# Holding weight casts behind convolution taps, value copies and the last head's scaling

## The chip, the cores and the metric

The kernel runs on one core of one Trainium2 chip. Its engines are TensorE (PE in the profile; PEld is its loading of stationary operands), VectorE (DVE), ScalarE (ACT), GpSimd (POOL) and SyncE (SP), each with its own queue of instructions, worked off in the order in which the program was laid out. The metric is the device time of one execution in microseconds (us): the median of three runs.

## The reference

One transformer-like block over 512 tokens of width 1024, in float32. After a root-mean-square norm, one large product with `w_in` gives the inputs of two mixers:

```python
qkv = jax.nn.silu(causal_depthwise_conv(jnp.concatenate([qa, ka, va], axis=-1), conv_a))
oa = chunk_gated_delta_rule(qa, ka, va, beta, g)            # 8 heads, keys of 128, values of 256
ya = (rmsnorm(oa, norm_a) * silu(za)) @ w_br_a
ob = chunk_retention(rotary(qb), rotary(kb) * (B_DK ** -0.5), vb)   # 4 heads, keys of 256, values of 512
yb = (rmsnorm(ob, norm_b) * silu(gb)) @ w_br_b
x = x + rmsnorm((sigmoid(gate_a) * ya + sigmoid(gate_b) * yb) @ w_out, n_mix_post)
hn = rmsnorm(x, n_mlp_pre)
return x + rmsnorm(jnp.square(relu(hn @ w_up)) @ w_down, n_mlp_post)
```

The convolution has four taps per channel: a channel's output is the sum of its last four inputs, each times a tap.

## The kernel before, in words

**Products in three parts.** Every large product takes both operands as a high part and a low part. A weight tile arrives from HBM by DMA as `raw` (128 x 1024, 512 KB, on SP's queue). `split_weights` (lines 152 to 164) turns it into `whi`, a cast on ScalarE (line 159), and `wlo`, what is left, a subtraction on VectorE (line 160). TensorE then makes three matmuls per pair of tiles: high by high, high by low, low by high. `raw` has two buffers (four in the stage of the second mixer), `whi` and `wlo` three each, so a cast waits for the DMA of its own load and for TensorE to be done with the load three before it. A "load" below is one such tile with its cast, its subtraction and its 24 matmuls of 512 columns.

**Who orders what.** Programs are written as if in sequence. A scheduler then lays each engine's queue out ahead of time, by readiness in its own model of time and by priority; `tc.high_priority(n)` moves an instruction n places forward. Weight casts and subtractions have 700 in the stage of the first mixer (`AHEAD`) and 200 elsewhere, the convolution's instructions 600 (`CONV_PRIO`), the recurrence 900. `tc.issue_after(ins)` puts the instructions of its block that run on the same engine as `ins` behind `ins` in that queue; instructions on other engines are not touched, and no semaphore is added. On TensorE most instructions of the first mixer keep the order of the program, which a small hand-written clock (`Clock`) lays out: chains of small work by due time, with the large products as fillers between.

**First mixer, about 40 to 480 us.** Fillers make keys, values, queries and gates from `w_in`. `product_features` uses two loads for two PSUM tiles of 128 channels by 512 tokens; when a tile's last matmul is made, `conv_silu` (line 917) takes it: tap 3 on ScalarE (line 923) from PSUM, taps 2, 1, 0 on VectorE (line 926), which also read PSUM, so that the bank comes free after the last of them; then Silu or Tanh. There are 8 tiles of keys, 16 of values and 8 of queries. The first four key tiles are made before the first load of the second four is split. Around that, base inverses of triangular blocks run on VectorE (lines 1081 and 1089), and the recurrence over four chunks per pair of heads alternates TensorE with VectorE (line 1359) and ScalarE (line 1375).

**Second mixer, about 480 to 880 us.** Per head, `scores` makes queries and keys and the scores; `values` makes value and gate with seven products of half-size blocks in place of eight (`seven`). `value` splits a row tile of the values: copy of the high part on ScalarE (line 1715), low part on VectorE (line 1716). `outputs` multiplies scores by values: 30 matmuls into four PSUM tiles over three banks, each read by line 1745 (VectorE) and line 1746 (ScalarE), and scales the four row tiles by the inverse norm (line 1751, ScalarE). The next head begins with the loads of its queries. After the last head, `gate_unit` runs another seven products for the second gate; between them `last_features` transposes the last head's output.

**Rest.** Output product, then the feed-forward part, again with seven products per block.

The functions that the change touches, and what calls them:

Of the kernel before, what the change touches and what calls it, by code (L numbers as in the profile page):

```python
# [14 lines left out]
AF = mybir.ActivationFunctionType  # L15
ALU = mybir.AluOpType
# [48 lines left out]
def hybrid_block_kernel(ctx: ExitStack, tc: tile.TileContext, a: dict, out: bass.AP):  # L65
    nc = tc.nc
# [9 lines left out]
    trickle, later_adds = [], []  # L76
    triples = []
    before, spent, queued, clocks = [None], [None], [JOBS_FROM], []
    ahead = [200]
    marks = []  # L80
    act = ctx.enter_context(tc.tile_pool(name="act", bufs=2))
    sm = ctx.enter_context(tc.tile_pool(name="sm", bufs=2))
# [69 lines left out]
    def split_weights(raw, n, nk, keep=None, ahead=200):  # L152
        if keep is None:
            hi = ring.tile([P, 1024], F32R, tag="whi", name="whi")
            lo = ring.tile([P, 1024], F32R, tag="wlo", name="wlo")
        else:
            hi, lo = keep
        with tc.high_priority(ahead):
            nc.scalar.copy(hi[:, :n], raw[:, :n])  # L159
            nc.vector.tensor_tensor(lo[:, :n], raw[:, :n], hi[:, :n], ALU.subtract)  # L160
# [325 lines left out]
    with tc.tile_pool(name="xp", bufs=2) as xp:  # L486
# [16 lines left out]
        for _ in range(2):  # L503
            w = act.tile([P, 2, D], F32R, tag="og", name="keep")
# [412 lines left out]
    def conv_silu(ps, ch, y, th=None):  # L917

        def tap(j):
            return convw[:, j * 32 + ch : j * 32 + ch + 1]  # L920

        with tc.high_priority(CONV_PRIO):
            nc.scalar.activation(y, ps, AF.Copy, scale=tap(3))
            for j in (2, 1, 0):
                s = 3 - j
                nc.vector.scalar_tensor_tensor(y[:, s:T], ps[:, 0 : T - s], tap(j), y[:, s:T], ALU.mult, ALU.add)  # L926
            if th is None:
                with tc.issue_after(exps[-1].ins):
                    nc.scalar.activation(y, y, AF.Silu, scale=2.0)
            else:  # L930
                nc.scalar.activation(th, y, AF.Tanh)
                nc.vector.scalar_tensor_tensor(y, th, 1.0, y, ALU.add, ALU.mult)
# [595 lines left out]
    with tc.tile_pool(name="pb", bufs=1) as pb_:  # L1528
# [180 lines left out]
            add(1, 0, a, new=True)  # L1709

        def values(h):
            vs, gs = [], []

            def value(t, p):
                nc.scalar.copy(vs[0][t], p)
                nc.vector.tensor_tensor(vs[1][t], p, vs[0][t], ALU.subtract)

            def gate(t):
                nc.scalar.activation(gs[0][:, t, :], gs[0][:, t, :], AF.Silu)

            parts = values_and_gates(vg_sums[h], gs, value, gate)
            next(parts)
            yield
            pairs = [[pb_.tile([P, 2, T], F32R, tag=f"vr{i}{x}", name="vr") for x in "ab"] for i in range(2)]
            vs += [[w[:, t, :] for w in pair for t in range(2)] for pair in pairs]
            gs.append(pb_.tile([P, 4, T], F32, tag="kr", name="gs"))
            for _ in parts:
                pass
            yield vs, gs[0]

        def outputs(scs, vs, gs):
            o = pb_.tile([P, 4, T], F32, tag="qr", name="o")
            ss = pb_.tile([P, 4], F32, tag="oss", name="oss")
            for j in (3, 2, 1, 0):
                ps = psx.tile([P, T], F32, tag="dl", name="dl", bufs=3)
                for i in range(j + 1):
                    js = slice((j - i) * P, (j - i + 1) * P)
                    mm3(
                        ps,
                        (scs[i][0][:, js], scs[i][1][:, js]),  # L1740
                        (vs[0][i], vs[1][i]),
                        i == 0,
                        i == j,
                    )
                nc.vector.tensor_tensor(o[:, j, :], ps, gs[:, j, :], ALU.mult)
                nc.scalar.activation(tmp("osq"), ps, AF.Square, accum_out=ss[:, j : j + 1])
            v = pb_.tile([P, 4], F32, tag="ov", name="ov")
            nc.vector.tensor_scalar(v, ss, 1.0 / 512, EPS, ALU.mult, ALU.add)
            rstd = rsqrt(v, 4, "b")
            for t in range(4):  # L1750
                nc.scalar.mul(o[:, t, :], o[:, t, :], rstd[:, t : t + 1])
            return Rows(None, lambda t, f: o[:, t, f * P : (f + 1) * P])

        def gate_unit(sums, gated, tag, between=None):
# [11 lines left out]
                if between:  # L1766
                    between(i)

        rows = None
        for h in range(4):  # L1770
            vals = values(h)
            scs = scores(h, rows, vals)
# [14 lines left out]
            rows = outputs(scs, *next(vals))  # L1787

        ya, gates, og = [], [], []
        for i in range(2):  # L1790
# [14 lines left out]
        def last_features(i):  # L1805
            if i == 0:
                og.extend(act.tile([P, 4, T], F32R, tag="og", name="og") for _ in range(2))
                return
            f = i - 1
            ps = psx.tile([P, 4, P], F32, tag="tr", name="tr", bufs=1)  # L1810
            with tc.issue_after(triples[-1].ins):
                for t in range(4):
# [387 lines left out]
```

## Time and profile before

| | us |
|---|---|
| median of three runs | 1322.16 (1319.62 to 1323.54) |
| profiled execution | 1322.3 |
| its span, first to last instruction | 1320.5 |
| TensorE busy | 1302.7 |
| VectorE busy | 928.1 |
| ScalarE busy | 698.3 |
| GpSimd busy | 114.5 |
| cast `whi` (line 159), one | 1.05 |
| subtraction `wlo` (line 160), one | 1.22 |

The page gives busy time, the chain of work that ended last and the costliest groups. The timeline has one row per instruction or run of equal instructions: start, time, engine, line, operation, out<-in, and in brackets the idle time of the engine just before it with what ended it. The chain in order of time has rows of start, time and what. The view of windows has a row per stretch: its length, then busy time of PE, PEld, DVE, ACT, POOL with the number of instructions, granted clock, share of the DMA engines and GB/s. TensorE's matmuls overlap, so the row of one lasts longer than its share of the pace; the pace is read from a run of many.

### The profile page before, as it was taken

Reading aid. Unit: us, or ns where it says so; the run is one execution under the profiler, and the core shown is the slowest. Engines: PE = TensorE matmul, PEld = TensorE weight load, DVE = VectorE, ACT = ScalarE, POOL = GpSimd, SP = SyncE. Lnnn points to the kernel's source line nnn. Section 1 sums busy time; section 2 is a strip of 40 time slices with the busy share of each in tenths; the row PEclk is TensorE's granted clock in tenths of the full one; section 3 lists DMA queues with packets and bytes.
Section 4 is the critical chain, followed back from the end, with each engine's and each line's share of the span. In section 5 each row is a group of like instructions: output and inputs, shape, how many; then the busy total and the mean of one; then the engine's idle time right before and its main releaser. Section 6 shows DMA issues by size and latency. Waiting matters only on the chain.

```text
span 1320.5 us, 17594 instructions
## 1 busy us (share of the span) xinstructions
PE 1302.7 (99%) x6555; PEld 1078.3 (82%) x6555; DVE 928.1 (70%) x1554; ACT 698.3 (53%) x1216; POOL 114.5 (9%) x119
## 2 busy tenths in 40 slices
PE   9999999999999999999999999999999999999997
PEld 7888787888888888878888888888889888888886
DVE  6889757486666567768769869769585736648478
ACT  5784546555533524555555554565266646355364
POOL 2101000000101100000010010100001110101001
PEclk9999999999999999999999999999999999999999
DMA  5336452466867867996895896875538895967335
GB/s 193 134 97 159 129 128 64 106 171 184 223 157 185 184 177 219 318 248 181 220 281 160 247 261 184 234 237 159 191 111 242 193 268 144 256 184 182 111 122 133
DMA packets 124149, 243.60 MB, mean 184 GB/s; under 512 B 7638, under 2 KB 39552, under 8 KB 123808
## 3 DMA queue, kind: packets, MB, share of 16 engines
q1 hardware_dynamic: 99808, 183.00, 42.7%
q0 software_dynamic: 21936, 53.12, 23.8%
q10 hardware_dynamic: 2320, 6.36, 1.3%
q8 instruction: 51, 0.84, 0.3%
q14 instruction: 34, 0.28, 0.1%
HBM read 237.20 MB, written 78.66 MB: 239 GB/s over the span
## 4 chain that ended last, share of the span: by engine, by line
PE 86%; DVE 6%; ACT 4%; DMA 2%; issue 1%; DVEq 0%; ACTq 0%
PE mm L692 17%; PE mm L340 16%; PE dl L340 15%; PE mm L97 8%; PE mm L95 8%; PE mm L96 8%; PE dl L692 5%; PE tr L421 1%; DVE wlo L160 1%; DMA raw<-in_w_in_dram 1%; PE tr L701 1%; PE dl L96 1%; PE dl L95 1%; PE dl L97 1%; PE mm L656 1%
## 5 line engine op out<-in xcount | busy, mean ns | idle before, releaser
L160 DVE TENSOR_TENSOR wlo<-raw,whi 128x1024 fp32r<-128x1024 f32 x230 | 281.0, 1223 | 187.9 <-ACT whi L159 187.0
L159 ACT CAST whi<-raw 128x1024 fp32r<-128x1024 f32 x230 | 241.7, 1052 | 269.4 <-PE mm L692 71.4
L692 PE MATMUL mm<-actT,whi 128*128 128x512 f32 x448 | 144.5, 403 | 0.0
L97 PE MATMUL mm<-hn,wlo 128*128 128x512 f32 (+1 forms) x288 | 105.4, 366 | 0.0
L96 PE MATMUL mm<-hn,whi 128*128 128x512 f32 (+1 forms) x288 | 105.3, 366 | 0.0
L95 PE MATMUL mm<-hn,whi 128*128 128x512 f32 (+1 forms) x288 | 105.3, 366 | 0.0
L692 PEld LDWEIGHTS mm<-actT,whi 128*128 128x128 f32 x448 | 80.6, 188 | 14.7
L692 PE MATMUL mm<-actT,wlo 128*128 128x512 f32 x224 | 87.7, 392 | 0.0
L160 DVE TENSOR_TENSOR wlo<-sum,whi 128x1024 fp32r<-128x1024 f32 x48 | 58.7, 1223 | 24.2 <-ACT whi L159 21.1
L159 ACT CAST whi<-sum 128x1024 fp32r<-128x1024 f32 x48 | 50.6, 1053 | 43.2 <-PE mm L340 21.1
L340 PE MATMUL dl<-whi,ffq 128*128 128x512 f32 x224 | 71.2, 389 | 0.0
L692 PE MATMUL mm<-whi,og 128*128 128x512 f32 x192 | 62.3, 397 | 0.0
L96 PEld LDWEIGHTS mm<-hn,whi 128*128 128x128 f32 x288 | 54.3, 189 | 8.8
L97 PEld LDWEIGHTS mm<-hn,wlo 128*128 128x128 f32 x288 | 54.3, 189 | 8.7
L95 PEld LDWEIGHTS mm<-hn,whi 128*128 128x128 f32 x288 | 54.3, 189 | 8.7
L340 PE MATMUL dl<-whi,xsum 128*128 128x512 f32 x192 | 61.3, 390 | 0.0
L692 PE MATMUL mm<-whi,actT 128*128 128x512 f32 x176 | 60.3, 404 | 1.0 <-DVE qf L926 1.0
L340 PE MATMUL mm<-whi,xsum 128*128 128x512 f32 x192 | 61.2, 390 | 0.0
L146 POOL DMA_DIRECT2D sums<-in_w_in_dram x28 | 32.3, 1154 | 330.4 <-DMA sums<-in_w_in_dram 322.7
L340 PE MATMUL dl<-whi,actT 128*128 128x512 f32 x192 | 60.9, 389 | 0.0
L340 PE MATMUL mm<-whi,ffq 128*128 128x512 f32 x192 | 60.9, 389 | 0.0
L1971 DVE TENSOR_TENSOR ffq<-r,ffq 128x512 fp32r<-128x512 f32 (+1 forms) x64 | 39.2, 622 | 28.0 <-ACT ffq L1971 27.9
(426 smaller groups left out, 3037.0 us busy)
## 6 DMA issues: line engine op xcount, KB each, us to landing
raw<-in_w_in_dram SPq DMA_DIRECT2D x95, 512.0 KB, 5.0
raw<-sums SPq DMA_DIRECT2D x58, 512.0 KB, 4.2
sums<-in_w_in_dram SPq DMA_DIRECT2D x44, 512.0 KB, 6.4
raw<-in_w_up_dram SPq DMA_DIRECT2D x36, 512.0 KB, 7.9
sums<-in_w_in_dram POOLq DMA_DIRECT2D x28, 512.0 KB, 8.5
sums<-sums POOLq DMA_DIRECT2D x26, 512.0 KB, 7.5
raw<-in_w_down_dram SPq DMA_DIRECT2D x18, 512.0 KB, 4.2
raw<-in_w_br_a_dram SPq DMA_DIRECT2D x16, 512.0 KB, 4.4
```

Of the source, the lines that this page charges most:

```text
L95: nc.tensor.matmul(ps, lh, rh, start=first, stop=False)
L96: nc.tensor.matmul(ps, lh, rl, start=False, stop=False)
L97: triples.append(nc.tensor.matmul(ps, ll, rh, start=False, stop=last))
L146: tc.keep_in_program_order(nc.gpsimd.dma_start(dst, src, accum_op=ALU.add))
L159: nc.scalar.copy(hi[:, :n], raw[:, :n])
L160: nc.vector.tensor_tensor(lo[:, :n], raw[:, :n], hi[:, :n], ALU.subtract)
L340: m = nc.tensor.matmul(pss[t], lhs[i // 2], rhs[i % 2], start=first and k + i == 0, stop=k + i == kts + 1, skip_group_check=not first,)
L421: nc.tensor.transpose(ps, src, ident)
L656: pin(nc.tensor.matmul(first_keys[f][:, 256:512], ws[w][:, kk, :], xs[x][:, 2 * j + kk, 256:512], start=False, stop=kk == 1 and i == 2, sk ...
L692: m = tc.keep_in_program_order(nc.tensor.matmul(*args, **kwargs))
L701: tc.keep_in_program_order(nc.tensor.transpose(ps, src, ident if by is None else by))
L1971: return nc.scalar.copy(dst[0], r), nc.vector.tensor_tensor(dst[1], r, dst[0], ALU.subtract)
```

## The change

A list `holds` collects pairs of an instruction on ScalarE and a count. Each call of `split_weights` goes through the list: where the count is zero, the cast is put behind that instruction on ScalarE's queue; every count falls by one, and pairs below zero go. Three places add to the list:

- each convolution: its tap 3, with count 1, so that the next load is let by and the one after it is held;
- each head's values: the last copy of a high part, with count 0, so that the next load is held;
- the last head: the last scaling on ScalarE, with count 0, added before the second gate's third product.

In the last head, the scaling of row tiles 0 and 1 moves to VectorE.

```diff
@@ split_weights
-        with tc.high_priority(ahead):
+        with ExitStack() as behind:
+            for hold in holds:
+                if not hold[1]:
+                    behind.enter_context(tc.issue_after(hold[0].ins))
+                hold[1] -= 1
+            holds[:] = [hold for hold in holds if hold[1] >= 0]
+            behind.enter_context(tc.high_priority(ahead))
             nc.scalar.copy(hi[:, :n], raw[:, :n])
             nc.vector.tensor_tensor(lo[:, :n], raw[:, :n], hi[:, :n], ALU.subtract)
@@ conv_silu
-            nc.scalar.activation(y, ps, AF.Copy, scale=tap(3))
+            holds.append([nc.scalar.activation(y, ps, AF.Copy, scale=tap(3)), 1])
@@ values
-                nc.scalar.copy(vs[0][t], p)
+                copied[:] = [nc.scalar.copy(vs[0][t], p)]
...
+            holds.append([copied[0], 0])
             yield vs, gs[0]
@@ outputs
-                nc.scalar.mul(o[:, t, :], o[:, t, :], rstd[:, t : t + 1])
+                w = o[:, t, :]
+                if last and t < 2:
+                    nc.vector.tensor_scalar(w, w, rstd[:, t : t + 1], None, ALU.mult)
+                else:
+                    scaled[:] = [nc.scalar.mul(w, w, rstd[:, t : t + 1])]
@@ last_features
             f = i - 1
+            if not f:
+                holds.append([scaled[0], 0])
```

More of the change, by code (lines that the diff above doesn't have):

```diff
@@ L78, in hybrid_block_kernel @@
     before, spent, queued, clocks = [None], [None], [JOBS_FROM], []
-    ahead = [200]
+    ahead, holds = [200], []
     marks = []
@@ L1711, in values @@
         def values(h):
-            vs, gs = [], []
+            vs, gs, copied = [], [], []
             def value(t, p):
-                nc.scalar.copy(vs[0][t], p)
+                copied[:] = [nc.scalar.copy(vs[0][t], p)]
                 nc.vector.tensor_tensor(vs[1][t], p, vs[0][t], ALU.subtract)
@@ L1728, in values, with outputs @@
                 pass
+            holds.append([copied[0], 0])
             yield vs, gs[0]
-        def outputs(scs, vs, gs):
+        def outputs(scs, vs, gs, last):
             o = pb_.tile([P, 4, T], F32, tag="qr", name="o")
@@ L1767, in gate_unit @@
                     between(i)
-        rows = None
+        rows, scaled = None, []
         for h in range(4):
@@ L1786, in hybrid_block_kernel @@
                 next(vals)
-            rows = outputs(scs, *next(vals))
+            rows = outputs(scs, *next(vals), h == 3)
         ya, gates, og = [], [], []
```

## The prediction

> **What bounds the kernel now.** I read the page first: engine shares, the chain that ended last, the costliest groups.
>
> ```profile
> span 1320.5 us, 17594 instructions
> ...
> PE 1302.7 (99%) x6555; PEld 1078.3 (82%) x6555; DVE 928.1 (70%) x1554; ACT 698.3 (53%) x1216; POOL 114.5 (9%) x119
> ...
> PE 86%; DVE 6%; ACT 4%; DMA 2%; issue 1%; DVEq 0%; ACTq 0%
> ...
> L160 DVE TENSOR_TENSOR wlo<-raw,whi 128x1024 fp32r<-128x1024 f32 x230 | 281.0, 1223 | 187.9 <-ACT whi L159 187.0
> L159 ACT CAST whi<-raw 128x1024 fp32r<-128x1024 f32 x230 | 241.7, 1052 | 269.4 <-PE mm L692 71.4
> ...
> raw<-in_w_in_dram SPq DMA_DIRECT2D x95, 512.0 KB, 5.0
> ```
>
> TensorE (PE) sets the time. ScalarE (ACT) has 47% idle, so moving a cast of 1.05 us is worth nothing by itself; it matters only where TensorE waits for what was queued behind that cast, or for the cast's own load. The chain in order of time gives the pace of TensorE:
>
> ```profile
> 38.35 3.06 PE mm L656 x24
> 41.41 6.83 PE mm L692 x30
> ...
> 542.69 10.88 PE dl L340 x48
> ```
>
> 10.88/48 = 0.227 us for a matmul of 512 columns, so a load's 24 matmuls last 5.44 us. A load of weights has three buffers: load C can be cast only when load X1, three before it, is used up, and is itself needed two loads later, 10.9 us. That is the slack which the change spends.
>
> **The change part by part.** Call the loads around a pair of convolution taps X0, X1 (whose products end the two PSUM tiles), then A, B, C. A hold with count 1 skips A and holds B. Before, B is cast when X0 ends, one load ahead of the taps; now behind the second tap. C was cast when X1 ends, just in front of the second tap. I take it that loads get their buffers in order, so that C follows B and the tap gets free of both. In all 15 loads are held for 32 taps, 4 for the value copies, 1 for the last scaling: 20 of 278. No instruction is added; two of 0.7 us change engine.
>
> *The first keys.* Four taps stand before the first two loads of the second keys, so the hold falls on the second of these, cast in an idle stretch so far.
>
> ```profile
> 28.21 1.98 ACT L159 CAST whi<-raw 128x1024 fp32r<-128x1024 f32 x2
> ...
> 46.37 0.67 ACT L923 ACTIVATE kf<-mm,convw 128x512 f32<-128x512 f32 x1
> 46.94 0.62 ACT L931 ACTIVATE th<-kf 128x512 f32<-128x512 f32 x1
> 47.46 1.03 ACT L159 CAST whi<-raw 128x1024 fp32r<-128x1024 f32 x1
> ...
> 46.71 0.62 PE L692 MATMUL mm<-actT,whi 128*128 128x512 f32 x2
> 47.17 0.39 PE L692 MATMUL mm<-actT,wlo 128*128 128x512 f32 x1
> ...
> 49.23 1.21 DVE L160 TENSOR_TENSOR wlo<-raw,whi 128x1024 fp32r<-128x1024 f32 x1
> ```
>
> The fourth tap runs at 46.37; TensorE wants this load from 46.71 and its low half from 47.17. Cast at 46.94 to 47.97, low half of 1.21 on VectorE (DVE) to 49.18: 2.0 us late. Bounds: 0, if the tap is issued as soon as its products end (38.35 + 3.06 = 41.41); 2.6, if the tanh goes first and the cast starts at 47.46. I take 2.0, since nothing in the change moves this tap forward. Queued behind the cast are the next loads' casts and the sums of squares; what they release is needed later by TensorE, which is itself late. Part is paid back, as TensorE later waits for VectorE in the same stage:
>
> ```profile
> PE dl L701 <- DVE acc L1044: 0.4, 1, 0.4
> ```
>
> Net +1.6.
>
> *The next keys* have the thinnest other margin. The last key tap, and the first use of the low half of the load that would be held behind it:
>
> ```profile
> 70.72 0.68 ACT L923 ACTIVATE kf<-mm,convw 128x512 f32<-128x512 f32 x1
> ...
> 73.66 0.39 PE L692 MATMUL mm<-actT,wlo 128*128 128x512 f32 x1
> ```
>
> 70.72 + 0.68 + 1.05 + 1.22 = 73.67: just on time if nothing stands between. I take +0.2, bounds 0 and 1.2 (one more low half ahead of it on VectorE).
>
> *The other 13 held loads of taps*: nothing. Cover is load A: 5.44 less 0.7 (tap), 1.05 and 1.22 leaves 2.5 us. If a 1.2 us operation stands ahead on both engines the cover is gone and each costs up to 1.2. Their raw buffers come free later too, so later loads on SP's queue, and the copies of partial sums behind them, are issued up to 5.4 us later; a load lands 5.0 us after its issue and is wanted about two loads, 10.9 us, after: covered. POOL's adds are not moved past anything.
>
> *Gate 0*, after the first query taps:
>
> ```profile
> 104.50 1.06 ACT L159 CAST whi<-raw 128x1024 fp32r<-128x1024 f32 x1 [2.68 <-PE mm L692]
> ...
> 110.86 1.05 ACT L159 CAST whi<-raw 128x1024 fp32r<-128x1024 f32 x1 [2.26 <-PE mm L692]
> 111.81 0.68 ACT L923 ACTIVATE qf<-mm,convw 128x512 f32<-128x512 f32 x1
> ...
> 112.51 1.22 DVE L160 TENSOR_TENSOR wlo<-raw,whi 128x1024 fp32r<-128x1024 f32 x1
> 113.64 0.75 DVE L926 SCALAR_TENSOR_TENSOR qf<-mm,convw,qf 128x511 f32<-128x511 f32 x1
> ...
> 116.17 0.47 PE L692 MATMUL mm<-whi,actT 128*128 128x512 f32 x1 [1.03 <-DVE qf L926]
> ```
>
> 104.50 is B, 110.86 is C. C's cast delays the tap by up to 0.95 and C's low half delays the VectorE taps by 1.13; TensorE waits 1.03 for the PSUM bank they free. With both behind the tap I take −1.0. Bounds: 0 (B's low half slips into the place of C's) and −1.2 (the wait and a restart).
>
> *The recurrence* at the third query pair:
>
> ```profile
> 212.19 1.05 ACT L159 CAST whi<-raw 128x1024 fp32r<-128x1024 f32 x1 [0.71 <-PE mm L692]
> ...
> 213.31 1.23 DVE L160 TENSOR_TENSOR wlo<-raw,whi 128x1024 fp32r<-128x1024 f32 x1
> 214.46 0.87 DVE L1359 SCALAR_TENSOR_TENSOR vt<-dl,neg_eg,vt 128x256 f32<-128x256 f32 x2
> ...
> 214.99 1.13 PE L692 MATMUL dl<-vt,rt 128*128 128x256 f32 x4 [0.88 <-DVE vt L1359]
> 216.69 1.21 PE L692 MATMUL dl<-vn,dall 128*128 128x256 f32 x3 [0.56 <-ACT vn L1375]
> ```
>
> TensorE waits for L1359, which waited for C's low half (214.46 − 213.31 = 1.15). Behind the tap, that low half comes after it: −1.1. But then B's and C's casts, 2.1 us, run on ScalarE where L1375 falls due, and a running cast isn't broken off: half of one, 0.5, is given back. −0.6; bounds −1.5 (both waits gone) and +1.0 (a whole cast in front, nothing won).
>
> *The value copies*, first head, and the windows of its 30 score-by-value matmuls and of the last head's:
>
> ```profile
> 587.62 1.05 ACT L159 CAST whi<-raw 128x1024 fp32r<-128x1024 f32 x1 [2.13 <-DMA raw<-in_w_in_dram]
> 588.57 0.58 ACT L1715 CAST vr<-dl 128x512 fp32r<-128x512 f32 x1
> ...
> 589.20 0.73 PE L95 MATMUL dl<-vr,s 128*128 128x512 f32 x2 [0.95 <-ACT vr L1715]
> ...
> 591.35 0.69 DVE L1745 TENSOR_TENSOR o<-dl,gs 128x512 f32<-128x512 f32 x1 [0.82 <-PE dl L97]
> ...
> 586.05:594.32 8.27, 7.32 (x32) 5.48 (x30) 4.13 (x6) 2.91 (x6) 0.09 (x1) 1.00 1.05 269
> 863.52:870.51 6.99, 6.99 (x31) 5.55 (x30) 4.12 (x6) 2.91 (x6) 0.00 (x0) 1.00 0.87 267
> sum 29.59, PE 28.64 PEld 22.01 DVE 16.50 ACT 11.63 POOL 2.10; mean PE 7.16 PEld 5.50 DVE 4.13 ACT 2.91 POOL 0.52
> ```
>
> Here the case is clean: a cast that waits 2.13 us for its DMA stands in front of the last copy, though the copy's PSUM is done when the window opens. Now the copy goes first. If all four heads come down to the last one's 6.99: 29.59 − 27.96 = −1.6. Bounds: −2.4 (30 × 0.227 = 6.80 each), and +0.8 with nothing won: copy from about 586.3 to 586.9, cast to 587.9, then three low halves in a row, 3 × 1.22, to 591.6, which is 0.2 after L1745's start at 591.35, and L1745 frees the PSUM of the next tile; 4 × 0.2. The held load itself is ready at 589.1 and wanted at 594.3.
>
> *The last head's scaling*, rows by operation (min/median/max ns) and the transposes that wait for it:
>
> ```profile
> L1751 ACT ACTIVATE o<-o,rs_y x16: 706/720/736, 598.4 to 881.0; 128x512 f32<-128x512 f32 x16
> L545 DVE TENSOR_SCALAR xn<-x,nr_y 128x512 f32<-128x512 f32 x7 | 3.2, 485 | 0.1
> ...
> 881.39 0.70 PE L421 MATMUL tr<-cmat,o 128*128 128x128 f32 x4
> ```
>
> Two of 0.72 leave ScalarE, two of about 0.485 (the nearest VectorE form) come to VectorE. Four transposes start every 0.11 us, without a wait: −0.1, bounds −0.1 and +1.2 (the held cast's low half late).
>
> **Sum:** +1.6 + 0.2 − 1.0 − 0.6 − 1.6 − 0.1 = −1.5. The profiled execution took 1322.3 (span 1320.5 and 1.8 around it), the median is 1322.16: I forecast 1320.7.
>
> **The rivals.** *Faster:* the fourth key tap is issued early and no held load is late. Then 0 − 1.2 − 1.1 − 2.0 − 0.1 = −4.4: 1317.8. For it: that tap's PSUM is free at 41.41, 5 us before it runs. Against: the tanh and exponentials before it on the same queue are untouched.
>
> *Slower:* held casts come too late, at B's first use. It decides from the point where the second tap runs more than 2.5 us after its product. Price 2.6 (first keys, nothing paid back) + 1.2 (next keys) + 1.2 at three more groups = 7.4; less 1.6 and 1.0 won: +4.8, 1327.0. For it: from 46 to 75 the rows of ScalarE stand without gaps, and in the delta rule VectorE is full. Against: 2.5 us of cover elsewhere.
>
> *No effect:* each wait removed reappears at the next, as with two chained waits at 214.99 and 216.69, and the key load is paid for by the copies: 1322.2.
>
> *A slower clock:* the granted clock is 1.00 in the windows above, across a wait of 0.95. Were it to halve for one load after a longer wait, its 24 matmuls would last 10.9 instead of 5.44: 1320.7 + 5.4 = 1326.1. The Trainium skill, page "TensorE: Matmul & The Clock Gate", section "Part 1: The HAM clock gate", says that TensorE's clock falls to half after an idle window of about 3.4 us; by that rule a late load of 2.0 or 2.6 us would not do it, and no row here shows a wait long enough to try it.
>
> **How the numbers follow.** Chances: forecast 0.44, faster 0.26, slower 0.12, no effect 0.16, clock 0.02. A measurement of this kernel tells about 0.3%, 4 us, from no change, so faster means below 1318.2, slower above 1326.1. Below lie about 6 tenths of the faster rival and a tail of the forecast (its terms' lower bounds sum to −5.2, 1317.0): 0.21; above, most of the slower one: 0.11. Range 1316.2 to 1326.0: below, 1317.0 less about half of what the three runs before lie apart from their median; above, the late loads up to most of the slower rival's price. About 0.1 is left out on each side.
>
> **What would show it.** Right: the row of L692 after the first 24 matmuls of the second keys (near 47) shows a wait for `whi` or `wlo`; the wait for `qf` near 116 is gone; the four windows of score-by-value matmuls are near 7.0; a copy L1715 stands before the first cast of the next head. Wrong: no wait near 47 (faster rival); new waits of matmuls for L160 at other held loads (slower); windows near 7.0 but the span unchanged (no effect); a tap still behind a cast, by which loads don't take buffers in order and the change doesn't do what it says.

## The result, and the profile after

The changed kernel takes 1354.06 us (median of five runs, 1352.25 to 1355.58) against 1322.16: the ratio on record, taken over the runs, is 1.0235, 95% interval 1.0222 to 1.0248. It is 31.9 us slower; forecast were 1320.7, and a range that ended at 1326.0.

The page of the changed kernel (lines after the diff have moved: cast L159 is now L165, low half L160 is L166, tap L923 is L929, matmul L692 is L698, transposes L701 are L707):

```profile
span 1353.8 us, 17577 instructions
...
PEclk9999799999999999999999999999999999999999
...
PE 77%; DVE 11%; ACT 5%; DMA 4%; issue 2%; DVEq 0%; ACTq 0%
...
raw<-in_w_in_dram SPq DMA_DIRECT2D x95, 512.0 KB, 5.8
```

The work is the same, but the chain leans on VectorE with 11% instead of 6% and on transfers with 4% instead of 2%, and one slice has a TensorE clock below full speed. The loss sits in one stage. TensorE runs its instructions in nearly the same order in both kernels, so the start of each can be set against its start before: the same matmul is 1.5 us later at 44 us of the kernel before (first matmuls, ahead of all edits), 15.2 at 152, 33.3 at 480, 33.1 at 1312, its last. Nearly everything is lost between 46 and 490 us of the changed kernel.

What TensorE waited for in this stage (us in total, times, longest), first before (to 460 us, where the same matmuls end), then after (to 490):

```profile
PE tr L701 <- DVE og L1444: 1.0, 1, 1.0
PE mm L692 <- DVE qf L926: 1.0, 1, 1.0
PE dl L692 <- DVE vt L1359: 0.9, 1, 0.9
```

```profile
PE tr L707 <- DVE og L1450: 8.1, 5, 2.1
PE dl L698 <- DVE vt L1365: 3.2, 2, 2.9
PE dl L698 <- DVE rn L1096: 3.0, 1, 3.0
PE mm L698 <- DVE tmp L1087: 2.0, 1, 2.0
PE mm L698 <- ACT whi L165: 1.1, 1, 1.1
PE tr L707 <- ACT vt L935: 1.1, 1, 1.1
PE mm L698 <- DVE wlo L166: 1.1, 2, 0.5
```

With the rows of 0.2 to 0.7 that follow in both, 4.4 us became 20.7: 16.3 more. Only 2.2 of that is a wait for a held load itself (`whi`, `wlo`). The rest is for other things that came late.

The other part of the loss is the clock. The rows below are stretches of 3.41 us (length, busy time and instructions of PE, PEld, DVE, ACT, POOL, granted clock, DMA share, GB/s), each pair a wait and what follows it:

```profile
119.30:122.71 3.41, 1.96 (x9) 1.30 (x7) 3.41 (x6) 1.02 (x2) 1.15 (x1) 1.00 0.36 44
122.71:126.13 3.42, 2.84 (x13) 2.36 (x13) 3.29 (x16) 0.63 (x1) 0.00 (x0) 1.00 1.00 168
150.02:153.43 3.41, 0.75 (x4) 0.29 (x2) 3.41 (x6) 0.00 (x0) 0.39 (x1) 1.00 0.60 113
153.43:167.09 13.66, 13.30 (x170) 9.51 (x170) 6.32 (x12) 7.77 (x13) 0.00 (x0) 0.50 0.18 50
310.45:313.86 3.41, 1.34 (x7) 0.80 (x7) 3.15 (x4) 1.62 (x3) 0.00 (x0) 1.00 0.47 138
313.86:317.27 3.41, 3.41 (x11) 2.82 (x10) 0.75 (x1) 0.69 (x1) 0.00 (x0) 0.50 0.86 283
477.70:481.11 3.41, 0.77 (x4) 0.65 (x5) 2.61 (x4) 1.35 (x5) 0.19 (x1) 1.00 0.71 197
481.11:484.53 3.42, 3.42 (x10) 2.70 (x9) 0.00 (x0) 2.05 (x5) 1.82 (x2) 0.50 1.13 303
```

Where TensorE was busy for 1.34 us or less of such a stretch, its clock is one half in the next; where it was busy for 1.96, it is not. (In the stretch from 47.6 us, that of the held key load, it was busy for 1.74, and the next was halved.) In this execution that happened six times: for 3.41 us from 51.0, 313.9, 419.7, 436.7 and 481.1 and for 13.65 us from 153.4. Half of 30.7 us is 15.4. Together 16.3 + 15.4 + 1.5 of the first matmuls = 33.2, against a difference of the spans of 33.3. That the sum closes so well is in part luck. Set against its start before, each matmul shows what a place cost: a half-clock stretch of 3.41 us cost 1.6 to 1.7, the one of 13.65 us only 5.0 and not 6.8, some 13 in all; and a wait of 2.07 set TensorE back by 2.2, one of 3.0 by 3.1.

**How a hold makes others late.** The timeline of ScalarE, then VectorE, then TensorE behind a pair of value taps of the changed kernel:

```profile
307.75 0.69 ACT L929 ACTIVATE vt<-mm,convw 128x512 f32<-128x512 f32 x1 [2.03 <-PE mm L698]
308.34 1.99 ACT L165 CAST whi<-raw 128x1024 fp32r<-128x1024 f32 x2
...
310.76 0.68 ACT L1448 ACTIVATE og<-tr,vecs 128x512 fp32r<-128x512 f32 x1
```

```profile
309.93 2.35 DVE L166 TENSOR_TENSOR wlo<-raw,whi 128x1024 fp32r<-128x1024 f32 x2
312.20 0.74 DVE L932 SCALAR_TENSOR_TENSOR vt<-mm,convw,vt 128x509 f32<-128x509 f32 x1
312.86 0.74 DVE L1450 SCALAR_TENSOR_TENSOR og<-tr,vecs,og 128x512 fp32r<-128x512 f32 x1
```

```profile
313.65 0.96 PE L707 MATMUL tr<-cmat,vt 128*128 128x128 f32 x4 [2.07 <-DVE og L1450]
```

VectorE at the same place in the kernel before, where one low half stood in front of a tap and `og`, and TensorE did not wait:

```profile
294.11 1.23 DVE L160 TENSOR_TENSOR wlo<-raw,whi 128x1024 fp32r<-128x1024 f32 x1 [0.54 <-ACT whi L159]
...
295.91 0.74 DVE L1444 SCALAR_TENSOR_TENSOR og<-tr,vecs,og 128x512 fp32r<-128x512 f32 x1
```

B's and C's casts now stand in one piece behind the tap, and so do their low halves on VectorE. In front of what waits behind them, that is 2.0 and 2.35 us: the last VectorE tap, and the two copies that empty the bank of the transposes (`og`, the gated output of the pair of heads before). The next transposes need that bank.

The second way goes through the transfers. A `raw` buffer whose cast is held stays full, SP's queue stands at the next load (near the last queries for up to 13.1 us, before the change up to 7.7), and the copies of partial sums behind it are issued close together afterwards. What ScalarE's casts waited for in this stage, before and after:

```profile
ACT whi L159 <- PE mm L692: 71.4, 38, 7.1
```

```profile
ACT whi L165 <- PE mm L698: 30.6, 15, 7.1
ACT whi L165 <- DMA raw<-in_w_in_dram: 19.6, 8, 5.3
```

Before, two casts of this stage waited for such a transfer, 2.5 us in all; now eight do, 19.6. With the other transfers into `raw` it was six casts and 9.7 us, and is fourteen and 30.4. Two stretches around the last queries, 18 and 26 us; the DMA engines' share is the last number but one:

```profile
433.00:451.00 18.00, 15.40 (x66) 12.00 (x65) 10.57 (x14) 5.37 (x8) 0.00 (x0) 0.91 0.17 58
451.00:477.00 26.00, 26.00 (x128) 21.78 (x127) 14.24 (x30) 8.21 (x25) 3.12 (x3) 1.00 0.97 231
```

At the same matmuls of the kernel before the shares were 0.64 and 0.96. So the second stretch is no fuller than it was; what is new is the nearly empty one ahead of it, whose transfers come later. The chain that ends in TensorE's wait of 2.93 at 480.3, in order of time:

```profile
462.21 14.68 DMA raw<-in_w_in_dram
...
476.99 1.05 ACT whi L165
...
479.21 0.68 DVE vt L1410
479.89 0.40 DVE vt L1365
```

A transfer of 512 KB took 14.7 us, issue to landing; the load at this place of the kernel before had taken 11.3 (issued at 432.35), and no cast waited for it. It was issued 1.2 us later against TensorE's work and took 3.4 longer. TensorE did not want this load yet. But its low half, laid out ahead of the recurrence's steps L1410 and L1365, kept VectorE standing for 3.4 us. The inverse met the same, here by a late issue: its load was issued at 121.38 in place of 107.67, about 7 us later against TensorE's work, and its cast ran 7.8 us after that. The low half behind it:

```profile
130.26 1.23 DVE L166 TENSOR_TENSOR wlo<-raw,whi 128x1024 fp32r<-128x1024 f32 x1 [4.15 <-ACT whi L165]
```

From the start of its first transpose on VectorE to that of its last it took 48.2 us (105.31 to 153.55) instead of 42.8 (99.67 to 142.46); 4.15 of the 5.4 are this one gap, and TensorE waited 3.0 for it at 153.8.

**The value copies** did most of what was forecast at their own place, and it went back close by. Windows of the 30 score-by-value matmuls, and VectorE in the first:

```profile
618.88:626.33 7.45, 7.45 (x34) 5.93 (x32) 6.14 (x8) 4.98 (x9) 1.14 (x1) 1.00 0.83 222
...
895.55:902.99 7.44, 7.08 (x31) 5.55 (x30) 6.13 (x8) 4.98 (x9) 0.00 (x0) 1.00 0.52 153
sum 29.78, PE 29.42 PEld 23.34 DVE 24.54 ACT 19.91 POOL 4.14; mean PE 7.35 PEld 5.83 DVE 6.14 ACT 4.98 POOL 1.03
```

```profile
620.65 3.50 DVE L166 TENSOR_TENSOR wlo<-raw,whi 128x1024 fp32r<-128x1024 f32 x3 [0.26 <-ACT whi L165]
624.07 1.88 DVE L1752 TENSOR_TENSOR o<-dl,gs 128x512 f32<-128x512 f32 x3
```

By length that is 29.78 in place of 29.59, but the windows don't hold the same work. In each of the first three, two matmuls of the next head's product (0.45 us) now stand in front of the last three of the 30. Without them these windows are 7.0 each, in place of 8.27, 7.28 and 7.05, and the wait for the first head's copy is gone. In the last head nothing could be put in front: its window grew from 6.99 to 7.44, as TensorE waited 0.36 there for a bank: its readers L1752 and, behind that, L1753 (the square on ScalarE) came late, because the low halves stand in one piece in front of L1752 (2.35 us in the last head, 3.5 in the first). Like for like the four windows came down by 1.2. But 0.3 went back some 8 us behind each of the first three, at the transposes of the head's output, and 0.7 at 916 us (before's time) in a wait for `tb`.

### The profile page after: what moved, and what is told of

It is laid out like the page before. It is cut to its first block, busy times and chain, and to the rows that moved or that the text cites. A ratio compares the mean times of both kernels' runs of the same rounds, so it can differ in the third digit from the quotient of the medians.

```text
span 1353.8 us, 17577 instructions
## 1 busy us (share of the span) xinstructions
PE 1320.0 (98%) x6555; PEld 1088.2 (80%) x6555; DVE 923.9 (68%) x1556; ACT 696.1 (51%) x1214; POOL 114.8 (8%) x119
## 4 chain that ended last, share of the span: by engine, by line
PE 77%; DVE 11%; ACT 5%; DMA 4%; issue 2%; DVEq 0%; ACTq 0%
PE mm L346 14%; PE mm L698 14%; PE dl L346 14%; PE mm L96 8%; PE mm L95 8%; PE mm L97 8%; PE dl L698 5%; DVE wlo L166 3%; DMA raw<-in_w_in_dram 2%; ACT whi L165 1%; PE tr L427 1%; PE dl L95 1%; PE tr L707 1%; PE dl L96 1%; PE dl L97 1%
## 5 line engine op out<-in xcount | busy, mean ns | idle before, releaser
L166 DVE TENSOR_TENSOR wlo<-raw,whi 128x1024 fp32r<-128x1024 f32 x230 | 279.1, 1221 | 161.9 <-ACT whi L165 159.1
L165 ACT CAST whi<-raw 128x1024 fp32r<-128x1024 f32 x230 | 239.5, 1051 | 232.0 <-PE mm L96 61.2
L698 PE MATMUL mm<-actT,whi 128*128 128x512 f32 x448 | 151.7, 421 | 1.1 <-ACT whi L165 1.1
L698 PEld LDWEIGHTS mm<-actT,whi 128*128 128x128 f32 x448 | 84.6, 198 | 17.4 <-ACT whi L165 1.6
L698 PE MATMUL mm<-actT,wlo 128*128 128x512 f32 x224 | 91.2, 407 | 0.5 <-DVE wlo L166 0.5
L166 DVE TENSOR_TENSOR wlo<-sum,whi 128x1024 fp32r<-128x1024 f32 x48 | 58.5, 1220 | 26.5 <-ACT whi L165 26.5
L165 ACT CAST whi<-sum 128x1024 fp32r<-128x1024 f32 x48 | 50.5, 1052 | 43.0 <-PE mm L346 20.5
L698 PE MATMUL mm<-whi,actT 128*128 128x512 f32 x176 | 60.4, 405 | 2.0 <-DVE tmp L1087 2.0
L698 PE MATMUL mm<-whi,og 128*128 128x512 f32 x192 | 62.3, 397 | 0.0
```

The source lines that it names most:

```text
L698: m = tc.keep_in_program_order(nc.tensor.matmul(*args, **kwargs))
```

## The experiments

All kernels below compute the whole block but for the two with stalls, which are kernels of their own. Ratios are to the kernel before, over the runs of both, with 95% intervals; the quotient of two medians can differ from them by 0.1%.

**Which part loses.** First the change without its line in `conv_silu`:

```diff
-            holds.append([nc.scalar.activation(y, ps, AF.Copy, scale=tap(3)), 1])
+            nc.scalar.activation(y, ps, AF.Copy, scale=tap(3))
```

> The change without the holds behind convolution taps: only the holds behind the value copies and the last scaling, and the two scalings on VectorE. Theory A: the whole loss of 32 us comes from the taps' holds, which put loads B and C on ScalarE and VectorE as a pair (1.99 and 2.35 us in one piece) in front of a convolution's last tap, the copies of og and the base inverse; TensorE then waits 1.3 to 3.2 us at some nine places between 46 and 485 us (about 16 us), and six of these waits are followed by a halved granted clock (five times 3.41 us, once 13.65: 15.4 us). Then this kernel takes 1320.6 (value copies -1.6) to 1322.2 (gain given back as after 869 us in the changed kernel), and no stretch before 1300 us has a granted clock of one half. Rival B, the holds of values and last head cost something too: over 1326.

Measured: 1322.62, ratio 1.0002 (0.9992 to 1.0012). The taps' line alone:

```diff
-            holds.append([copied[0], 0])
...
-                if last and t < 2:
+                if False:
...
-                holds.append([scaled[0], 0])
+                pass
```

> Only the holds behind convolution taps, count 1 as in the change; no hold behind value copies and last scaling, all four scalings on ScalarE. Theory A: 1354 to 1356, with the same waits between 46 and 485 us and about 15 us at half clock. Rival B: under 1345.

Measured: 1353.8, ratio 1.0238 (1.0217 to 1.026). So the whole loss is the taps', and copies and last scaling are worth nothing measurable either way. In the trace without taps no stretch between 40 and 1300 us is at half clock. Its matmuls run 0.4 us later than before at 580 us, 0.8 earlier at 596, behind the first head's window, and 0.6 later from 920 us on. The 1.2 won at the first head all went back: 0.3 near 602 us, 0.2 near 778, 0.5 near 870 and 0.6 near 916.

**Whose taps.** The hold under a condition, the rest of the change kept:

```diff
+            if ch >= 16:        # values; queries: ch < 8; keys: 8 <= ch < 16
+                holds.append([first_tap, 1])
```

> The whole change, with holds behind the values' taps only (16 of 32 taps). By the places of the waits in the changed kernel: 95.5 (0.8), the inverse at 153.8 in part (up to 3.1 and 6.8 of half clock), the four at og (8.0 and 5.1 of half clock): 1336 to 1347. If keys and queries carry the loss: under 1330.

> The whole change, with holds behind the queries' taps only (8 of 32). By the places of the waits in the changed kernel: the wait at 123.3 is 1.0 longer than the 1.03 before, the wait in the recurrence at 215 shorter: 1322 to 1325. By the prediction's terms (gate 0 -1.0, recurrence -0.6): 1321. If it also makes the wait for a late transfer at 480.3 (3.1 and 1.7 of half clock): 1327 to 1330.

> The whole change, with holds behind the keys' taps only (8 of 32). The parts add up: no taps 1322.6, values +17.6, queries +10.6, all 1354.1, which leaves +3.3 for the keys: 1325 to 1327, with waits of 1.3 for whi and 0.7 for wlo at the first use of the held load near 48 us, and a half clock behind them where they fall into one window. By the prediction's term (+1.6 and +0.2): 1324. If it also carries the inverse's wait: over 1329.

Measured: values 1340.21, ratio 1.0132 (1.0119 to 1.0146); queries 1333.22, 1.0084 (1.0061 to 1.0107); keys 1326.78, 1.0034 (1.0022 to 1.0047). The three add up to 2.5%, the taps alone cost 2.4%. Values and keys came within what was expected. In the keys' run TensorE waits 1.2 for `whi` and then for `wlo`, with one half-clock stretch of 3.41 behind it: 3.8 us in all at this place, and 0.7 more by 95 us, which is not paid back. The queries cost more than expected, even with the late transfer (1327 to 1330): TensorE waits 2.2 at 117 us (1.0 before) and 2.2 at 154 us (0.3 before), with 3.41 us at half clock behind the second, and 4.2 for the late transfer with 6.8 us at half clock. Without holds at the last pair of queries:

```diff
+            if ch < 6:
+                holds.append([first_tap, 1])
```

> The queries' taps as in the run of queries only (1333.2), but without holds behind the two taps of the last pair of heads. There TensorE waited 4.9 longer than before at 457 us for a low half whose load came late by DMA, with 6.8 of half clock behind it. Theory G: the held casts keep both raw buffers, SP's queue stands at the next load with four partial-sum copies behind it, and these then crowd the DMA engines, so that a load issued 10 us ahead is late; the wait and the half clock go, 1322 to 1326. Rival: the transfers are late because of what the earlier pairs' holds did to SP's queue, 1331 to 1334.

Measured: 1324.68, ratio 1.0019 (1.0008 to 1.0031). The wait of 4.2 and its half clock are gone, so the late transfer belongs to the holds of the pair next to it. The medians differ by 8.5 us; in the trace of the queries' run this place alone cost 7.3, and the wait at 154 us is shorter here too.

**One held load or two.** The count 2 lets A and B by and holds C alone:

```diff
-            holds.append([nc.scalar.activation(y, ps, AF.Copy, scale=tap(3)), 1])
+            holds.append([nc.scalar.activation(y, ps, AF.Copy, scale=tap(3)), 2])
```

> The whole change, but the taps' count is 2 in place of 1: the hold lets A and B by and holds C alone, which was cast right in front of the second tap before. Theory A, the pair is what costs: without it 1319 to 1323 (the forecast's gains at gate 0 and in the recurrence, -1.6, and the first keys free). Rival C, any cast put behind a tap is late for its own first use or blocks ScalarE's queue: half of the loss or more stays, 1338 to 1354.

Measured: 1327.8, ratio 1.0048 (1.003 to 1.0066). Of the 31.9 us, 26 go with B: no wait for a transfer at 480, none for the inverse, no half clock before the end. The rest is more than expected (1319 to 1323): theory A was right on the main part and too kind on the rest: with C alone the waits for `og` are still 4.2 in all, up to 1.2 each (one low half of 1.22 in front), and there is one of 1.7 in the second keys.

**What stands in front of the copies.** `og`'s two copies with a priority above the casts' and low halves':

```diff
+                with tc.high_priority(1000):
                     nc.scalar.activation(hi, ps.rearrange("p t c -> p (t c)"), AF.Copy, scale=scale)
...
```

> The whole change, with the copies of og (high part on ScalarE, low part on VectorE) given a priority above the casts' and low halves', so that at the waits of 313.7, 330.3, 419.5 and 436.2 us of the changed kernel they stand between B's cast and C's and ahead of the low halves. Theory A, the pair of casts and of low halves in front of them makes TensorE wait there: the four waits (1.0 to 2.1 us) and the half clock behind three of them go, 1342 to 1348. Rival F, the copies are late because ScalarE stands at a tap that waits for TensorE: nothing moves, 1352 to 1356.

Measured: 1348.78, ratio 1.0193 (1.017 to 1.0216). No wait for `og` is left among the seven longest, so they were late through the order on their own queues and not through TensorE. But 5 us were won and not 6 to 12: in this execution the waits for L1365 are 9.2 in three, in place of 3.2 in two. At the new one the order is

```profile
347.16 1.23 DVE L166 TENSOR_TENSOR wlo<-raw,whi 128x1024 fp32r<-128x1024 f32 x1 [5.92 <-ACT whi L165]
348.30 0.87 DVE L1365 SCALAR_TENSOR_TENSOR vt<-dl,neg_eg,vt 128x256 f32<-128x256 f32 x2
```

with the cast waiting 5.75 for its transfer. The one at the last queries grew from 2.9 to 5.0. TensorE comes earlier here and waits longer for the late loads.

**Cast or low half.** The change binds the cast on ScalarE; the low half's place on VectorE is left to its priority of 700, above the taps' 600. Here a hold also puts the low half behind the tile's last VectorE tap:

```diff
                     behind.enter_context(tc.issue_after(hold[0].ins))
+                    for step in hold[2:]:
+                        behind.enter_context(tc.issue_after(step.ins))
...
-            holds.append([nc.scalar.activation(y, ps, AF.Copy, scale=tap(3)), 1])
+            holds.append([first_tap, 1, step])
```

> The whole change, but a hold behind a tap also puts the load's low half behind that tile's last tap on VectorE; the change itself binds ScalarE's queue alone, and the low halves (priority 700) went ahead of the last taps (600). Theory H, the order on VectorE is what the prediction had wrong at gate 0: TensorE's wait for the bank of the second query tile, 2.03 us at 123.3 in the changed kernel, goes or falls under 0.5. The copies of og still stand behind the low halves, so the four waits there stay at 1 to 2.5 us, and so do the late transfer and the half clock: 1346 to 1353. Rival, the low halves are then late for their own matmuls: new waits for wlo, 1354 or more.

Measured: 1360.38, ratio 1.0283 (1.0267 to 1.0299). The time is the rival's. Theory H was right at its place, as the wait of 2.03 at gate 0 is gone, but the waits for `wlo` went from 1.1 to 5.9 in total and that for the inverse from 3.0 to 4.5. Held longer, the loads are late for their own matmuls.

**The clock by itself.** A kernel of bursts and waits, the cause of the half clock apart from this change:

> A kernel of its own, which computes nothing of the reference: TensorE makes bursts of 62, 66 and 71 matmuls of 128x512, 14 to 16 us each, and ahead of each burst waits for one VectorE operation of 512 to 4096 columns, about 0.7 to 4.4 us; then three more waits of about 3.3 us, each followed by four groups of one matmul of 512 columns, 32 small ones of 32x32 and two of 512, as at 153.8 us of the changed kernel. Theory D, by the profile after: the clock is granted in windows of 3.41 us on a fixed grid, and a window in which TensorE was busy for less than about 0.55 of it halves the next; then waits under 1.5 us never halve it, waits of 2 us do in some positions, waits over 3.3 us always, and one busy window brings it back, but not while the small matmuls run. Rival E: only an idle time of a whole window or more halves it, so nothing under 3.4 us does, and the halved stretches of the changed kernel come from something else.

VectorE's operations were twice as fast as I had assumed, so the longest wait was 2.39. Among the 30 in front of full bursts one halved the clock, with 2.19 of its 2.39 us in one window; up to 1.59 in a window never did. Hence the second kernel:

> As the kernel with stalls, which computes nothing of the reference: now two VectorE operations ahead of each burst, for waits of about 1.4 to 3.6 us in three positions each; then, without any wait, 3, 6 and 12 groups of one matmul of 512 columns, 32 of 32x32 and two of 512, each followed by 60 of 512. Theory D, the window of 3.41 us: idle time of up to 1.6 within one window leaves the clock, of 1.9 and more halves the next window, for one window where full bursts follow; a wait of 2 to 3 us that lies across two windows can leave it. The groups of small matmuls halve nothing by themselves if only waiting counts, and do if a small matmul counts as idle. Rival E: only waits of 3.4 us and more halve it.

TensorE's waits there, and the windows around two of them:

```profile
60.70 1.80 PE L83 MATMUL mm<-z,w 128*128 128x512 f32 x5 [1.98 <-DVE z L95]
...
148.73 3.48 PE L83 MATMUL mm<-z,w 128*128 128x512 f32 x14 [3.18 <-DVE z L95]
```

```profile
58.14:61.55 3.41, 1.43 (x7) 0.88 (x6) 1.85 (x2) 0.00 (x0) 1.00 0.00 0
61.55:64.96 3.41, 3.41 (x10) 2.67 (x9) 0.00 (x0) 0.00 (x0) 0.50 0.02 5
...
143.47:146.88 3.41, 2.08 (x10) 1.39 (x8) 1.29 (x1) 0.00 (x0) 1.00 0.00 0
146.88:150.30 3.42, 1.57 (x7) 1.31 (x8) 1.76 (x2) 0.00 (x0) 1.00 0.00 0
```

Here a wait of 1.98 inside one window halved the next one, and a wait of 3.18 that lay across two did nothing. In all 30, idle time of up to 1.68 us within a window never halved it, from 1.90 on always, and the five between, 1.78 to 1.88, went both ways. In the block the mark is as blurred: 3.41 - 1.74 = 1.67 did halve it at 47.6 us of the changed kernel, and 3.41 - 1.51 = 1.90 did not at 115.4 us of the queries' run. It lies a little under 2 us, and is not sharp in these records. Every half-clock stretch starts on one grid of 3.413 us, in this kernel as in the changed one (51.03, and 30 windows later 153.43). Theory D holds, rival E falls. The small matmuls also halve the clock, without any wait: three groups gave 10.2 us at half clock, six 27.3, twelve 54.6. This is the likely reason why the stretch from 153.4 was so long, 13.65 us: the products with the inverse are 32x32.

Then the clock in the change itself: 23 matmuls that nobody reads, inside four of its waits.

```diff
+    def fill(n):
+        ps = psx.tile([P, T], F32, tag="dl", name="fill", bufs=3)
+        for _ in range(n):
+            tc.keep_in_program_order(
+                nc.tensor.matmul(ps, xs[1][:, 0, 0:P], xs[0][:, 0, :], start=True, stop=True)
+            )
...
+            if turns[0] in (112, 144, 160):
+                fill(5)
...
             p1 = [bank(16) for _ in range(2)]
+            fill(8)
```

> The whole change, with 23 matmuls of 512 columns that nobody reads added on TensorE just ahead of four of its waits: 8 ahead of the first product with the base inverse (153.8 us of the changed kernel, a wait of 3.0), 5 each ahead of the three transposes that waited 2.07 us at 313.7, 419.5 and 436.2. They last 1.8 and 1.1 us, less than the waits, so the work behind them starts when it did. Theory D, a window of 3.41 us with TensorE busy for less than half halves the next window's clock: these windows are now busy for 0.55 or more, the half clock there is gone (13.65 and three times 3.41 us in the profile), and the time falls by up to 12 us, to 1342 to 1349 (in runs where some of the three did not halve the clock anyway, less is won). Rival E, the clock has another cause or the halved stretches cost nothing: 1354 to 1358.

Measured: 1349.07 (1341.58 to 1351.15), ratio 1.0193 (1.0168 to 1.0217): 5 us faster than the change with more work in it. At the inverse and at `og`:

```profile
149.22 1.98 PE L695 MATMUL fill<-actT 128*128 128x512 f32 x8
151.97 0.69 PE L707 MATMUL dl<-rn,acc 32*32 32x32 f32 x32 [0.78 <-DVE rn L1108]
...
306.84 1.29 PE L695 MATMUL fill<-actT 128*128 128x512 f32 x5
309.07 0.66 PE L719 MATMUL tr<-cmat,vt 128*128 128x128 f32 x4 [0.94 <-DVE og L1463]
```

The work behind the fill starts about when it did: 3.0 and 2.5 us after the matmul in front of the fill, against 3.4 and 2.5 in the changed kernel. The half clock behind all four is gone; only 3.41 us from 162.7, in the small products, are left there. So it was TensorE's idleness in these windows that halved the clock. Of the 5 us, the trace shows more at the four places and less elsewhere. Matmul by matmul, 3.2 were won at the inverse, where a wait of 1.2 for `mrb` comes in now, and 1.6 at each `og`; 2.0 more by 55 us, where the grid of this execution lay otherwise and nothing was halved. Back went 0.6 in the second keys and 4.2 at the late transfer (a wait of 5.8 instead of 2.9, and 6.8 us at half clock instead of 3.4).

**What is left of the gain.** What was worth having by these runs: C alone, behind the queries' taps, and the hold behind the first head's copies.

```diff
+            if ch < 8:
+                holds.append([first_tap, 2])
...
+            if not h:
+                holds.append([copied[0], 0])
```

> What was worth having, by the runs so far, without the rest: holds behind the queries' taps only, with count 2 (C alone, as in the run with count 2, whose wait in the recurrence at 215 us was 0.8 shorter), and the hold behind the first head's value copies alone (its window of 30 matmuls went from 8.27 to 7.44, those of the other heads grew by 0.17 to 0.45); nothing on keys, values and the last head. Theory: -0.8 at 215, -0.8 at 589, 0 to -1.0 at 116: 1319.6 to 1321. Rival, each is paid back at the next wait as in the run without taps: 1322 to 1323.

Measured: 1321.18, ratio 0.9992 (0.998 to 1.0003). The recurrence's wait became 0.6 shorter, but that at gate 0 is still 1.02, since C's low half slips between the taps on VectorE. The first head's window won 1.2. But the second head has no hold here, and there the same fault appears: a cast that waits 2.77 us for its transfer stands in front of the last copy, TensorE waits 1.58 for it at 680.8, and 1.6 us go back (in the kernel before, that cast waited 1.13 and TensorE not at all). So leaving out the other heads' holds, which the growth of their windows had suggested, was not free. With the low half held behind the last tap as well (the edit of the run on cast or low half, with count 2):

> As the run with the queries' C alone and the first head's copies (1321.2, where TensorE still waited 1.02 us at 116.2 because C's low half stood between the second tile's taps on VectorE), with that low half put behind the last tap as well. Theory H: the wait at 116.2 goes: 1320.2. Rival: it comes back as a wait for wlo, or the inverse on VectorE is pushed back by as much: 1321 to 1322.5.

Measured: 1321.03, ratio 0.9982 (0.9971 to 0.9993). The wait at gate 0 is gone (the matmul starts 1.1 earlier there); 1.3 go back at a wait for `vt` near 345 us. It is the only one of these kernels whose interval lies below 1, by 0.9 to 3.8 us; from the run before it, at 1321.18, it can't be told, and one small gain among so many kernels is weak evidence.

## Why the prediction was wrong, step by step

- **The load behind the tap (wrong, and it decided).** "I take it that loads get their buffers in order, so that C follows B and the tap gets free of both" came out: the two casts stand as a pair. The error was to price the pair only at its own first use. "The other 13 held loads of taps: nothing" asked whether `whi` and `wlo` come in time, and they nearly do (2.2 us of waits in all). It did not ask what stands behind 2.0 us of casts on ScalarE and 2.35 us of low halves on VectorE. There stood `og`'s copies (8.1 us of waits instead of 1.0) and the last tap of gate 0's tile. The taps' holds as a whole cost 31, and 26 of it went when B was let by. "In the delta rule VectorE is full" was said of the held loads alone.
- **The transfers (wrong).** "A load lands 5.0 us after its issue and is wanted about two loads after: covered" took a median for a bound, and let the copies of partial sums be merely later. One load of the kernel before had already taken 11.3, at the very place where one now took 14.7. That a late load also stops VectorE, whose low half for it stands in front of the inverse and the recurrence, was not in the working. With its half clock, the one at the last queries cost 7.3 us in the trace of the queries' run.
- **The first keys (size right, price wrong).** Forecast: 2.0 late, with the wait "near 47", net +1.6. It came: idle for 1.1 for `whi` and 0.5 for `wlo`, which set TensorE back by 2.1. But a half clock of 1.7 follows, which the sum lacked. The wait for `acc` that was to be paid back is gone in the changed kernel (0.6), yet 1.0 is lost at 95.5 for `vt`; in the keys' run it stays. The keys cost 4.2 in the runs.
- **The next keys**: +0.2 forecast, and no wait at this load.
- **Gate 0 (wrong).** −1.0 forecast, +1.0 came: 1.03 became 2.03. The bound of 0, "B's low half slips into the place of C's", named the reason; it was both of them, so the bound was too kind. With the low half held too the wait vanished, so the forecast's −1.0 was the price of an edit that the change does not make.
- **The recurrence (right).** −0.6 forecast; the taps alone, C alone and the query version gave −0.6, −0.8 and −0.6 there.
- **The value copies (right at their place, wrong in sum).** −1.6 forecast. The copies stand ahead of the casts as forecast, and like for like the windows came down by 1.2. But by 920 us TensorE is 0.3 later, set against the kernel before, than it was ahead of the first window: the gain went back behind the windows and in the last head, where the low halves in a row did what was kept as the far bound ("to 591.6, which is 0.2 after L1745's start"). The forecast priced the windows and not the next wait.
- **The last head**: −0.1 forecast, and the two scalings on VectorE took 0.48 each, as estimated. In the trace TensorE wins 0.1 at these transposes; no run could tell it.
- **The rivals.** The slower one, at 1327.0, had the wrong place: it looked for late loads at their own first use. The clock was held to be out of reach ("no row here shows a wait long enough to try it"), with a chance of 0.02 and a price of 5.4. It came six times and cost 13 to 15. A late load of 2.0 to 2.6 us "would not do it" by the rule of the Trainium skill cited there; here idle times of 1.67 and 2.07 us within a window did. The two rivals were treated as cases apart, when most of the longer waits bring their own half clock. One reading behind the slower rival was wrong too: "from 46 to 75 the rows of ScalarE stand without gaps", where ScalarE was idle for 1.7 us at 61.5 and for 1.8 at 68.1.
- **The signs.** Of the four signs of being right two came, the wait for `whi` at the second keys and the copies ahead of the casts. The windows came near 7.0 in three heads of four, and the wait near 116 grew. The sum missed all the same, because no sign looked at what stands behind a held load.

## What to carry to other kernels

Price a moved instruction by what is queued behind its new place on every engine that it feeds, and by the buffer that it keeps, not by its own slack: here the held loads were in time and their neighbours were not. A tie on one queue does not tie the follower on the next; if the second half has a higher priority it goes in front of the very work that was to be protected. A wait on TensorE of about 2 us or more may cost nearly twice its length, through the clock of the window after it: the waits of 2.07 for `og` cost up to 3.9 each.

## What the runs showed of the hardware

TensorE's clock is granted in windows of 3.413 us on a grid that runs on by itself. In the traces here a window with 1.96 us or more of idle time halved the next each time; one with 1.66 or less did not unless small matmuls followed or filled it; between the two both happened. One window of full 512-column work brings the clock back. A window that is itself at half clock needs less idle time to keep it there: in the second kernel of bursts 0.76 and 0.84 us did (from 529.2 and 573.6 us), 0.23 (from 78.6) did not. The Trainium skill, page "TensorE: Matmul & The Clock Gate", section "Part 1: The HAM clock gate", gives the same free-running window of 3413 ns, and the runs agree. That section of the Trainium skill puts the fall at an idle window of about 3.4 us, and there the runs differ: a little over half a window was enough, and a wait of 3.18 across two windows did nothing.

Work of 32x32 matmuls did not hold the clock: with TensorE busy throughout, it fell to one half in the second window of the small groups, stayed there while they lasted and came back behind them.

```profile
594.03:597.44 3.41, 3.41 (x85) 2.96 (x83) 0.00 (x0) 0.00 (x0) 1.00 0.02 5
597.44:600.85 3.41, 3.41 (x51) 3.22 (x49) 0.00 (x0) 0.00 (x0) 0.50 0.00 0
```

In the kernel before, similar groups of the inverse ran from 143.5 us at full clock; what keeps them above the mark there was not tried.

Where a wait lies on the grid differs from execution to execution. Counted from the first instruction, the half-clock stretches start 0.5 us past a multiple of 3.413 in the run of the values' taps, 2.3 past it with the fill and 3.25 in the changed kernel. So the same wait halves the clock in one execution and not in another: with the taps alone, the waits of 2.07 for `og` near 420 and 435 us lay across two windows (1.87 us of idle time in one, 1.58 in the other case), and did not. This fits the spread of the runs with many waits (1341.6 to 1351.2 with the fill) against that of the kernel without taps (1321.3 to 1323.8).
